# The beginning of a one-core transformer layer: who sums the tokens' squares, who copies the spread rows, and the order of the first loads

## The chip, the cores and the metric

The kernel runs on one core of one Trainium2 chip. The core has five engines, each with an instruction queue of its own that is worked off in order: TensorE (PE, matrix products; PEld are its weight loads), VectorE (DVE), ScalarE (ACT), GpSimd (POOL) and SyncE (SP), which here issues nearly all transfers from device memory. The metric is the device time of one execution in microseconds (us), the median of several runs. A profile shows one execution.

## The reference, cut to what matters

One layer with two token mixers and a gated MLP, on 512 latent tokens (`x`) and 256 context tokens (`ctx`), width 2048, everything in float32. What matters for this change is the modulated RMS norm ahead of the input projection:

```python
sc_ = jax.nn.silu(c)
scc = jax.nn.silu(c_ctx)
mod_x = (sc_ @ w_ada[l] + b_ada[l])[:, None, :]
mod_c = (scc @ w_ada[l] + b_ada[l])[None, None, :]
sh1, s1, g1, sh2, s2, g2 = jnp.split(mod_x, N_MOD, axis=-1)
sh1c, s1c, g1c, sh2c, s2c, g2c = jnp.split(mod_c, N_MOD, axis=-1)
...
h = _modulate(_rmsnorm(x, norm1_w[l]), sh1, s1)      # xn * (1 + s1) + sh1
hc = _modulate(_rmsnorm(xc, norm1_w[l]), sh1c, s1c)
q_da, k_da, v_da, q_mla, k_mla, v_mla = _mixer_inputs(h, tabs, *proj)
...
def _rmsnorm(x, w):
    xf = x.astype(jnp.float32)
    y = xf * lax.rsqrt(jnp.mean(xf * xf, axis=-1, keepdims=True) + EPS)
    return y.astype(x.dtype) * w
```

So each token needs the sum of its 2048 squares, and each of the 2048 features needs a shift and a scale for each of the two conditions `c` and `c_ctx`: products of `w_ada` with the two vectors.

## The kernel before, in words

Features lie on the 128 partitions, tokens along the free axis: `x_t[kt]` is feature tile kt (0 to 15) of the 512 latent tokens, `ctx_t` holds two tiles of the 256 context tokens in each block. A float32 product is made from three products of a high part (`wh`, `hh`) and a low part (`wl`, `hl`): `mm3`, lines 104 to 106.

The beginning, up to the first projection products, goes like this:

- Rows (lines 192 to 201). The two conditions are loaded as one row each, ACT takes their SiLU, PE multiplies a column of ones with the row (L199, four pieces of 512 for each condition), which spreads it over all partitions, and DVE copies the result from PSUM into `cb` and `ccb` (L200). Then ACT loads the function table that holds logarithm and exponential (`exp_ln_tables`, shown as L155).
- Squares (L266 to L284). For each feature tile, ACT squares the 512 latent columns (L276) and the 256 context columns (L277) into a tile `sq` of 768 columns. Even tiles are added to `sqs` by DVE (L279); odd tiles are summed over the partitions by PE with a matrix of ones into the PSUM tile `ssq` (L282, each set being products over 512 and 256 columns); at the end PE sums `sqs` as well (L284). The tag `h` has three buffers: `sqs` keeps one, so two turn.
- Root (`rstd`, L159 to L164). ACT takes logarithm and exponential, DVE corrects the result by one Newton step: `rinv`, one number for each token.
- Modulation, in rounds u of two feature tiles. `scales(u)` loads four blocks `adak` (0.5 MB each, four buffers) and multiplies them on PE with the conditions (`products`, L219), with a copy on ACT (L221), two small products (L223) and the result in `a1` (L235). `shifts(kt)` loads `ada[kt]` in two halves (0.5 MB each, five buffers). For even kt, DVE multiplies and sums each half with `cb` and `ccb`: four instructions (L251; the trace shows CUSTOM_DVE_ANT_0), the first half's and then the second half's, into one column of `modx` and `modc`. For odd kt, PE transposes the block (L258), ACT copies it (L259), and `products` does the rest (L262). `acc` is one PSUM bank that scales and odd shifts share.
- Projection. `w_g0[kt]` is loaded and split by ACT (L80) and DVE (L81). For each kt, DVE makes `h` from x, `a1` and `rinv` (L330), ACT adds the shift and keeps the high part (L332), DVE makes the low part (L333), and PE multiplies (L104 to L106). Round u + 1 of the modulation runs beside the products of round u.

After that stage (until about 183 us) come the other features, attention, the output projection and the MLP, which the change doesn't touch.

The order of the instructions on each engine is not that of the source. A planner fixes it before the run: it steps through a model of the engines and lets each one take, of the instructions that it holds ready, the one of the highest priority, which is that of the earliest line unless a block is marked `tc.high_priority()`. `tc.keep_in_program_order(i)` pins one instruction behind the instruction that was written last before it for the same engine; it isn't held back otherwise. On the chip each queue is then in order: an instruction that waits holds up all that stand behind it.

Of the kernel before, what the change touches and what calls it, by code (L numbers as in the profile page):

```python
# [9 lines left out]
F32 = mybir.dt.float32  # L10
# [3 lines left out]
ALU = mybir.AluOpType  # L14
# [3 lines left out]
P = 128  # L18
D = 2048
KT = D // P  # L20
T = 512
C = 256
TT = T + C
# [29 lines left out]
def layer_kernel(ctx: ExitStack, tc: tile.TileContext, small, rope, c_row, cc_row, x_t, ctx_t, ada, ada_k,  # L53
                 w_g0, w_f, w_v, w_uqn, w_uqr, w_ukv, w_o, w_up0, w_up, w_dn, out_t):
    nc = tc.nc
    pe, ve, sc, gp = nc.tensor, nc.vector, nc.scalar, nc.gpsimd
# [8 lines left out]
    def nm(s):  # L65
        n[0] += 1
        return f"{s}{n[0]}"

    def s_tile():
        return ps_s.tile([P, 1024], F32, tag="s", name=nm("s"))  # L70
# [3 lines left out]
    def b_tile(tag="b", bufs=None):  # L74
        return ps_b.tile([P, 512], F32, tag=tag, name=nm(tag), bufs=bufs or nb[0])

    def split(dst_h, dst_l, src, scale=None):

        if scale is None:
            sc.copy(dst_h, src)  # L80
            ve.tensor_tensor(dst_l, src, dst_h.bitcast(F32), op=ALU.subtract)  # L81
        else:
            sc.mul(dst_h, src, scale)
            ve.scalar_tensor_tensor(out=dst_l, in0=src, scalar=scale, in1=dst_h.bitcast(F32),
                                    op0=ALU.mult, op1=ALU.subtract)

    def wblock(src, cols=1024, pool=None):
        pool, full = (pool, cols) if pool else (wp, 1024)
        raw = pool.tile([P, full], F32, tag="wr", name=nm("wr"), bufs=3 if full == 1024 else 2)
        nc.sync.dma_start(raw[:, :cols], src)  # L90
        hi = pool.tile([P, full], F32R, tag="wh", name=nm("wh"), bufs=3)
        lo = pool.tile([P, full], F32R, tag="wl", name=nm("wl"), bufs=3)
        split(hi[:, :cols], lo[:, :cols], raw[:, :cols])
        return hi, lo
# [25 lines left out]
    def col(name, j=0):  # L120
        o = OFF[name] + j
        return smt[:, o:o + 1]
# [3 lines left out]
    ones32 = cst.tile([P, P], F32, name="ones32")  # L126
# [27 lines left out]
    def exp_ln_tables():  # L154
        tc.keep_in_program_order(sc.preload_act_table_set("natural_log_exp_and_others"))  # L155

    def rstd(out, ssq, dim, t1, t2):

        sc.activation(out, ssq, AF.Ln, bias=epst, scale=1.0 / dim)  # L159
        sc.activation(out, out, AF.Exp, scale=-0.5)  # L160
        ve.tensor_scalar(out=t1, in0=ssq, scalar1=1.0 / dim, scalar2=EPS, op0=ALU.mult, op1=ALU.add)
        ve.scalar_tensor_tensor(out=t2, in0=out, scalar=-0.5, in1=out, op0=ALU.mult, op1=ALU.mult)
        ve.tensor_tensor(t2, t2, t1, op=ALU.mult)
        ve.scalar_tensor_tensor(out=out, in0=t2, scalar=1.5, in1=out, op0=ALU.add, op1=ALU.mult)  # L164
# [12 lines left out]
    def a2k(dt=F32):  # L177
        return ap_.tile([P, 512], dt, tag="a2k", name=nm("a2k"))
# [3 lines left out]
    def c2k(dt=F32):  # L182
        return hcp.tile([P, 512], dt, tag="c2k", name=nm("c2k"))

    st = tc.alloc_tile_pool(name="st", bufs=1, reuse_waits="tile")
# [8 lines left out]
    for row, wide in ((c_row, cb), (cc_row, ccb)):  # L194
        nc.sync.dma_start(wide[0:1], row)
        sc.activation(wide[0:1], wide[0:1], AF.Silu)
        for j in range(0, D, 512):
            t = b_tile()
            pe.matmul(t, ones32[0:1], wide[0:1, j:j + 512], start=True, stop=True)  # L199
            ve.tensor_copy(wide[:, j:j + 512], t)  # L200
    exp_ln_tables()

    sel = sm.tile([P, 2], F32, name="sel")
# [9 lines left out]
    def products(src, n):  # L213
# [8 lines left out]
        for i in range(n // P):  # L222
            pe.matmul(acc[:, 2 * i:2 * i + 2], row[:, i * P:(i + 1) * P], sel, start=True, stop=True)  # L223

    def scales(u):

        ws = []
        for j in range(4):
            wk = st.tile([P, 4, 2 * P], F32, tag="adak", name=nm("adak"), bufs=4)
            nc.sync.dma_start(wk, ada_k[u, j // 2][:, (j % 2) * 4:(j % 2) * 4 + 4])  # L230
            ws.append(wk)
        products(lambda kt: ws[kt // 4][:, kt % 4], 2 * P)
        for i in range(2):
            kt = 2 * u + i
            ve.tensor_scalar(out=a1[:, 2 * kt:2 * kt + 2], in0=acc[:, 2 * i:2 * i + 2], scalar1=b1[:, kt:kt + 1],  # L235
                             scalar2=col("n1", kt), op0=ALU.add, op1=ALU.mult)

    def shifts(kt):


        ws = []
        for hf in range(2):
            w = st.tile([P, D // 2], F32, tag="ada", name=nm("ada"), bufs=5)
            nc.sync.dma_start(w, ada[kt][:, hf * D // 2:(hf + 1) * D // 2])
            ws.append(w)
        dst = [m[:, kt:kt + 1] for m in (modx, modc)]
        if kt % 2 == 0:
            for hf, w in enumerate(ws):
                for i, (vec, d) in enumerate(zip((cb, ccb), dst)):
                    t = w if i else st.tile([P, D // 2], BF16, tag="junk", name=nm("junk"), bufs=1)  # L250
                    ve.tensor_tensor_reduce(out=t, in0=w, in1=vec[:, hf * D // 2:(hf + 1) * D // 2], op0=ALU.mult,  # L251
                                            op1=ALU.add, scale=1.0, scalar=d if hf else col("b_ada", kt), accum_out=d)
            return
        wt = st.tile([P, KT, P], F32, tag="wt", name=nm("wt"), bufs=1)
        for q in range(4):
            for i in range(4):
                k = (q % 2) * 4 + i
                pe.transpose(acc[:, i * P:(i + 1) * P], ws[q // 2][:, k * P:(k + 1) * P], ident)  # L258
            sc.copy(wt[:, 4 * q:4 * q + 4].rearrange("p k f -> p (k f)"), acc)  # L259
        products(lambda kt: wt[:, kt], P)  # L260
        for i, d in enumerate(dst):
            ve.tensor_scalar(out=d, in0=acc[:, i:i + 1], scalar1=col("b_ada", kt), scalar2=None, op0=ALU.add)  # L262

    ssq = s_tile()
    sqs = st.tile([P, TT], F32, tag="h", name="sqs", bufs=3)
    xs, cs = [], []  # L266
    for kt in range(KT):
        xt = a2k()
        nc.sync.dma_start(xt, x_t[kt])
        xs.append(xt)  # L270
        if kt % 2 == 0:
            ct = c2k()
            nc.sync.dma_start(ct, ctx_t[kt // 2])
            cs.append(ct)
        sq = sqs if kt == 0 else st.tile([P, TT], F32, tag="h", name=nm("sq"), bufs=3)
        sc.square(sq[:, :T], xt)  # L276
        sc.square(sq[:, T:], cs[-1][:, (kt % 2) * C:(kt % 2 + 1) * C])  # L277
        if kt % 2 == 0 and kt:
            ve.tensor_tensor(sqs, sqs, sq, op=ALU.add)  # L279
        elif kt:  # L280
            for c0, c1 in ((0, T), (T, TT)):
                pe.matmul(ssq[:, c0:c1], ones32, sq[:, c0:c1], start=kt == 1, stop=False)  # L282
    for c0, c1 in ((0, T), (T, TT)):
        pe.matmul(ssq[:, c0:c1], ones32, sqs[:, c0:c1], start=False, stop=True)  # L284
    rinv = st.tile([P, TT], F32, name="rinv")
    nt2 = st.tile([P, TT], F32, tag="h", name="nt2", bufs=3)
    rstd(rinv, ssq[:, :TT], D, sqs, nt2)
    g0w = []

    def modulation(u):  # L290
        scales(u)
        for kt in (2 * u, 2 * u + 1):
            shifts(kt)
            g0w.append(wblock(w_g0[kt], 640, st))

    modulation(0)
    nc.sync.dma_start(silu_c, cb[0:1])
    nc.sync.dma_start(ropet, rope)
# [4 lines left out]
    for i in range(2):  # L303
        o = OFF["lam"] + 128 * i
        ve.tensor_tensor_reduce(out=lt, in0=smt[:, o:o + 64], in1=smt[:, o + 64:o + 128], op0=ALU.mult,
                                op1=ALU.add, scale=1.0, scalar=0.0, accum_out=ls[:, i:i + 1])
# [9 lines left out]
    for kt in range(KT):  # L316
        if kt % 2 == 0 and kt < KT - 2:
            modulation(kt // 2 + 1)
        ct = cs[kt // 2][:, (kt % 2) * C:(kt % 2 + 1) * C]
# [5 lines left out]
        with tc.high_priority():  # L325
            h = st.tile([P, TT], F32, tag="h", name=nm("h"), bufs=3)
            for i, (x, c, m, (hh, hl)) in enumerate(((xs[kt], slice(0, T), modx, hx[kt]),
                                                     (ct, slice(T, TT), modc, hc[kt]))):
                b, t, r = m[:, kt:kt + 1], h[:, c], rinv[:, c]
                ve.scalar_tensor_tensor(out=t, in0=x, scalar=a1[:, 2 * kt + i:2 * kt + i + 1], in1=r,  # L330
                                        op0=ALU.mult, op1=ALU.mult)
# [3 lines left out]
        for f in range(5):  # L335
            w = (wh[:, f * P:(f + 1) * P], wl[:, f * P:(f + 1) * P])
# [81 lines left out]
    for i in range(2):  # L418
        t = kv.tile([P, TT], F32, tag="lt", name=nm("ckv"), bufs=3)
# [27 lines left out]
    for i in range(3):  # L447
        lat = b_tile()
        feature(lat, None)
        t = kv.tile([P, TT], F32, tag="lt", name=nm("cq"), bufs=3)[:, :T]  # L450
# [4 lines left out]
    for half in range(2):  # L455
        s0, s1, b0, b1_ = s_tile(), s_tile(), b_tile(), b_tile()
        vo = [s0[:, :512], s0[:, 512:], s1[:, :512], s1[:, 512:], b0, b1_]
        for kb in range(8):
            wh, wl = next_block()
            for j in range(2):  # L460
                kt = kb * 2 + j
                w = (wh[:, j * 512:(j + 1) * 512], wl[:, j * 512:(j + 1) * 512])
                for t in range(NKEY):
                    src, o = (hx[kt], t * P) if t < 4 else (hc[kt], (t - 4) * P)
# [164 lines left out]
    for h in range(NH):  # L629
        i = h % 2  # L630
# [3 lines left out]
        for qt in range(NQT):  # L634
            c = slice(qt * P, (qt + 1) * P)
# [44 lines left out]
    for dt in range(KT):  # L680
        ve.scalar_tensor_tensor(out=a2[:, dt:dt + 1], in0=modx[:, 64 + dt:65 + dt], scalar=1.0,
                                in1=col("n2", dt), op0=ALU.add, op1=ALU.mult)
# [24 lines left out]
    for g in range(3):  # L707
# [5 lines left out]
        for kb in range(8):  # L713
            if g:
                next_gemv(wo, 1)
            w = wblock(w_o[g, kb])
# [19 lines left out]
    for ft in range(3, NFT):  # L736
        for k in range(7):
            jobs.append(("p", ft, k))
            c, n_ = ft // FC, (ft % FC) * 7 + k
# [46 lines left out]
    hf, hx, t1, t2, t3, t4 = ([None] * KT for _ in range(6))  # L786
# [599 lines left out]
```

## Time and profile before

| | us |
|---|---|
| median of three runs | 2444.63 (2444.59 to 2448.08) |
| the profiled execution | 2446.12 |
| its span | 2444.3 |

| engine | busy, share of the span |
|---|---|
| PE | 97% |
| PEld | 81% |
| DVE | 71% |
| ACT | 46% |
| POOL | 9% |

How to read the views: a group or an instruction is given with its engine, the source line (L276 is line 276), the operation, what it writes and reads with their shapes, and its time; where an engine stood idle before it, the releaser of the wait follows an arrow. In the chain of waits, each row is a piece of the work that ended last, found by going back from the end. `issue` is time for which the profile shows no wait. Queues of transfers are shown as SPq where SP issues them. The beginning up to 60 us is 2.5% of the span.

### The profile page before, as it was taken

Reading aid. Unit: us, or ns where it says so; the run is one execution under the profiler, and the core shown is the slowest. Engines: PE = TensorE matmul, PEld = TensorE weight load, DVE = VectorE, ACT = ScalarE, POOL = GpSimd, SP = SyncE. Lnnn points to the kernel's source line nnn. Section 1 sums busy time; section 2 is a strip of 40 time slices with the busy share of each in tenths; the row PEclk is TensorE's granted clock in tenths of the full one; section 3 lists DMA queues with packets and bytes.
Section 4 is the critical chain, followed back from the end, with each engine's and each line's share of the span. In section 5 each row is a group of like instructions: output and inputs, shape, how many; then the busy total and the mean of one; then the engine's idle time right before and its main releaser. Section 6 shows DMA issues by size and latency. Waiting matters only on the chain.

```text
span 2444.3 us, 32956 instructions
## 1 busy us (share of the span) xinstructions
PE 2374.6 (97%) x12790; PEld 1987.4 (81%) x12790; DVE 1730.4 (71%) x2304; ACT 1116.3 (46%) x1700; POOL 221.0 (9%) x244
## 2 busy tenths in 40 slices
PE   7999999999999999999999999999999999999998
PEld 3778887877777778889888888888888888888887
DVE  4668786388868877369766666666666666666667
ACT  4342121155545542245545454545454545454545
POOL 0000000121100002100111111111111111111110
PEclk9999999999999999999999999999999999999999
DMA  7867899555411139523555555565556555555573
GB/s 276 275 238 293 308 339 325 178 179 138 140 59 44 44 147 332 176 87 113 137 140 135 141 135 142 134 143 133 143 132 143 133 141 134 140 135 141 133 191 106
DMA packets 130708, 403.33 MB, mean 165 GB/s; under 512 B 14323, under 2 KB 25075, under 8 KB 122099
## 3 DMA queue, kind: packets, MB, share of 16 engines
q1 hardware_dynamic: 104118, 350.87, 43.8%
q0 software_dynamic: 25280, 49.30, 11.6%
q8 instruction: 100, 1.64, 0.3%
q10 hardware_dynamic: 1152, 1.05, 0.1%
q14 instruction: 58, 0.48, 0.1%
HBM read 331.68 MB, written 69.48 MB: 164 GB/s over the span
## 4 chain that ended last, share of the span: by engine, by line
PE 83%; DVE 8%; ACT 3%; DMA 3%; issue 2%; POOL 1%; SPq 0%; DVEq 0%; ACTq 0%; POOLq 0%
PE y L1105 12%; PE b L104 10%; PE b L105 10%; PE b L106 10%; PE z L1105 6%; PE y L1107 6%; PE z L1107 3%; PE s L104 3%; PE s L105 3%; PE s L106 3%; PE s L482 3%; PE x L1105 2%; DMA ada<-in_ada 1%; PE x L1107 1%; PE f L104 1%
## 5 line engine op out<-in xcount | busy, mean ns | idle before, releaser
L961 DVE TENSOR_TENSOR wl<-wr,wh 128x1024 fp32r<-128x1024 f32 x144 | 176.4, 1225 | 157.1 <-ACT wh L953 156.5
L953 ACT CAST wh<-wr 128x1024 fp32r<-128x1024 f32 x144 | 151.0, 1049 | 233.3 <-PE b L105 119.5
L104 PE MATMUL b<-ah,wh 128*128 128x512 f32 (+1 forms) x664 | 256.8, 387 | 0.0
L105 PE MATMUL b<-al,wh 128*128 128x512 f32 (+1 forms) x664 | 256.7, 387 | 0.0
L106 PE MATMUL b<-ah,wl 128*128 128x512 f32 (+1 forms) x664 | 255.8, 385 | 0.0
L1126 POOL DMA_DIRECT2D x_d<-xs x160 | 139.7, 1003 | 1161.1 <-ACT xs L1125 1158.7
L961 DVE TENSOR_TENSOR wl<-rb,wh 128x1024 fp32r<-128x1024 f32 x123 | 150.1, 1220 | 126.8 <-ACT wh L953 126.8
L953 ACT CAST wh<-rb 128x1024 fp32r<-128x1024 f32 x123 | 129.3, 1051 | 188.3 <-PE b L105 116.1
L961 DVE TENSOR_TENSOR wl<-ws,wh 128x1024 fp32r<-128x1024 f32 x123 | 150.2, 1221 | 89.7 <-ACT wh L953 89.7
L80 ACT CAST wh<-wr 128x1024 fp32r<-128x1024 f32 (+3 forms) x102 | 99.1, 972 | 219.1 <-PE b L106 61.7
L171 DVE CUSTOM_DVE_ANT_0 ada<-ada,cb,smt 128x2048 f32<-128x2048 f32 x64 | 153.4, 2397 | 59.3 <-DMA ada<-in_ada 59.0
L953 ACT CAST wh<-ws 128x1024 fp32r<-128x1024 f32 x123 | 128.2, 1042 | 129.7 <-DVE ws L915 48.6
L1105 PE MATMUL y<-a2k,wh 128*128 128x512 f32 x656 | 164.0, 392 | 0.0
L81 DVE TENSOR_TENSOR wl<-wr,wh 128x1024 fp32r<-128x1024 f32 (+3 forms) x102 | 118.0, 1157 | 53.4 <-ACT wh L80 53.1
L104 PE MATMUL b<-a2k,wh 128*128 128x512 f32 (+1 forms) x376 | 141.7, 377 | 5.9 <-ACT a2k L810 4.3
L106 PEld LDWEIGHTS b<-ah,wl 128*128 128x128 f32 x664 | 124.8, 188 | 25.7
L104 PEld LDWEIGHTS b<-ah,wh 128*128 128x128 f32 x664 | 125.1, 188 | 22.9
L105 PEld LDWEIGHTS b<-al,wh 128*128 128x128 f32 x664 | 125.1, 188 | 22.0
L105 PE MATMUL b<-a2k,wh 128*128 128x512 f32 (+1 forms) x376 | 140.5, 374 | 0.0
L106 PE MATMUL b<-a2k,wl 128*128 128x512 f32 (+1 forms) x376 | 139.3, 371 | 0.0
L1105 PEld LDWEIGHTS y<-a2k,wh 128*128 128x128 f32 x656 | 118.6, 189 | 21.6
L1105 PE MATMUL y<-b2k,wh 128*128 128x512 f32 x410 | 107.8, 393 | 0.0
(449 smaller groups left out, 5770.7 us busy)
## 6 DMA issues: line engine op xcount, KB each, us to landing
ada<-in_ada SPq DMA_DIRECT2D x64, 1024.0 KB, 6.7
rb<-in_w_up SPq DMA_DIRECT2D x123, 512.0 KB, 4.5
wr<-in_w_dn SPq DMA_DIRECT2D x88, 512.0 KB, 4.2
x_d<-xs POOLq DMA_DIRECT2D x160, 256.0 KB, 5.9
wr<-in_w_up SPq DMA_DIRECT2D x53, 512.0 KB, 4.2
wr<-in_w_f SPq DMA_DIRECT2D x34, 512.0 KB, 6.4
adak<-in_ada_k SPq DMA_DIRECT2D x32, 512.0 KB, 6.0
ada<-in_ada SPq DMA_DIRECT2D x32, 512.0 KB, 6.4
```

Of the source, the lines that this page charges most:

```text
L80: sc.copy(dst_h, src)
L81: ve.tensor_tensor(dst_l, src, dst_h.bitcast(F32), op=ALU.subtract)
L104: pe.matmul(out, st[0], mv[0], start=start, stop=False, **kw)
L105: pe.matmul(out, st[0], mv[1], start=False, stop=False, **kw)
L106: pe.matmul(out, st[1], mv[0], start=False, stop=stop, **kw)
L171: ve.tensor_tensor_reduce(out=junk, in0=w, in1=vec, op0=ALU.mult, op1=ALU.add, scale=1.0, scalar=col("b_ada", j), accum_out=dst[:, j:j + 1])
L482: pe.matmul(s[:, c0:c1], a, b[:, c0:c1], start=i == 0, stop=i == len(mms) - 1)
L953: sc.copy(t, raw[:, k * n_:k * n_ + n_])
L961: ve.tensor_tensor(t, raw[:, k * n_:k * n_ + n_], hi[k].bitcast(F32), op=ALU.subtract)
L1105: pe.matmul(o, w[j][0], hs[j], start=start and j == 0, stop=False, skip_group_check=True)
L1107: pe.matmul(o[:, h0], w[j][1], hs[j][:, h0], start=False, stop=j == 7, skip_group_check=True)
L1126: gp.dma_start(x1_d[dt], x, accum_op=ALU.add)
```

## The change

- The eight copies of the spread rows (`cb`, `ccb`) go from DVE to ACT; the table load, pinned behind what was written before it on ACT, now comes behind the last of them.
- The square of the context columns goes from ACT to DVE. DVE adds tiles 1 to 13 to `sqs` (before: the even tiles 2 to 14); PE sums only `sqs` and the tiles 14 and 15. The loop and its loads are marked as of high priority, and the loads are pinned in written order.
- The first shift (`shifts(0)`) is written ahead of the root and ahead of `scales(0)`; its loads come before those of `scales(0)`, and its first instruction on DVE is pinned behind the last square. The root is marked as of high priority and gets two scratch tiles of its own.
- In the later rounds the even shift is written ahead of the scales; before, the scales came first.

```diff
         for j in range(0, D, 512):
             t = b_tile()
             pe.matmul(t, ones32[0:1], wide[0:1, j:j + 512], start=True, stop=True)
-            ve.tensor_copy(wide[:, j:j + 512], t)
+            sc.copy(wide[:, j:j + 512], t)
     exp_ln_tables()
...
+    def load(i, dst, src):
+        t = nc.sync.dma_start(dst, src)
+        if i == 0:
+            tc.keep_in_program_order(t)
+
     def scales(u):
...
-            nc.sync.dma_start(wk, ada_k[u, j // 2][:, (j % 2) * 4:(j % 2) * 4 + 4])
+            load(u, wk, ada_k[u, j // 2][:, (j % 2) * 4:(j % 2) * 4 + 4])
...
-            nc.sync.dma_start(w, ada[kt][:, hf * D // 2:(hf + 1) * D // 2])
+            load(kt, w, ada[kt][:, hf * D // 2:(hf + 1) * D // 2])
...
-                    ve.tensor_tensor_reduce(out=t, in0=w, in1=vec[:, hf * D // 2:(hf + 1) * D // 2], op0=ALU.mult,
-                                            op1=ALU.add, scale=1.0, scalar=d if hf else col("b_ada", kt), accum_out=d)
+                    r = ve.tensor_tensor_reduce(out=t, in0=w, in1=vec[:, hf * D // 2:(hf + 1) * D // 2], op0=ALU.mult,
+                                                op1=ALU.add, scale=1.0, scalar=d if hf else col("b_ada", kt),
+                                                accum_out=d)
+                    if kt == hf == i == 0:
+                        tc.keep_in_program_order(r)
...
-    for kt in range(KT):
-        xt = a2k()
-        nc.sync.dma_start(xt, x_t[kt])
-        xs.append(xt)
-        if kt % 2 == 0:
-            ct = c2k()
-            nc.sync.dma_start(ct, ctx_t[kt // 2])
-            cs.append(ct)
-        sq = sqs if kt == 0 else st.tile([P, TT], F32, tag="h", name=nm("sq"), bufs=3)
-        sc.square(sq[:, :T], xt)
-        sc.square(sq[:, T:], cs[-1][:, (kt % 2) * C:(kt % 2 + 1) * C])
-        if kt % 2 == 0 and kt:
-            ve.tensor_tensor(sqs, sqs, sq, op=ALU.add)
-        elif kt:
-            for c0, c1 in ((0, T), (T, TT)):
-                pe.matmul(ssq[:, c0:c1], ones32, sq[:, c0:c1], start=kt == 1, stop=False)
-    for c0, c1 in ((0, T), (T, TT)):
-        pe.matmul(ssq[:, c0:c1], ones32, sqs[:, c0:c1], start=False, stop=True)
-    rinv = st.tile([P, TT], F32, name="rinv")
-    nt2 = st.tile([P, TT], F32, tag="h", name="nt2", bufs=3)
-    rstd(rinv, ssq[:, :TT], D, sqs, nt2)
+    with tc.high_priority():
+        for kt in range(KT):
+            xt = a2k()
+            tc.keep_in_program_order(nc.sync.dma_start(xt, x_t[kt]))
+            xs.append(xt)
+            if kt % 2 == 0:
+                ct = c2k()
+                tc.keep_in_program_order(nc.sync.dma_start(ct, ctx_t[kt // 2]))
+                cs.append(ct)
+            sq = st.tile([P, TT], F32, tag="h", name=nm("sq"), bufs=3) if kt else sqs
+            c = cs[-1][:, (kt % 2) * C:(kt % 2 + 1) * C]
+            sc.square(sq[:, :T], xt)
+            ve.tensor_tensor(sq[:, T:], c, c, op=ALU.mult)
+            if kt and kt < KT - 2:
+                ve.tensor_tensor(sqs, sqs, sq, op=ALU.add)
+            if kt == KT - 3:
+                for c0, c1 in ((0, T), (T, TT)):
+                    pe.matmul(ssq[:, c0:c1], ones32, sqs[:, c0:c1], start=True, stop=False)
+            elif kt >= KT - 2:
+                for c0, c1 in ((0, T), (T, TT)):
+                    pe.matmul(ssq[:, c0:c1], ones32, sq[:, c0:c1], start=False, stop=kt == KT - 1)
     g0w = []
 
     def modulation(u):
+        if u:
+            shifts(2 * u)
         scales(u)
-        for kt in (2 * u, 2 * u + 1):
-            shifts(kt)
-            g0w.append(wblock(w_g0[kt], 640, st))
-
+        g0w.append(wblock(w_g0[2 * u], 640, st))
+        shifts(2 * u + 1)
+        g0w.append(wblock(w_g0[2 * u + 1], 640, st))
+
+    shifts(0)
+    with tc.high_priority():
+        rinv = st.tile([P, TT], F32, name="rinv")
+        nt1, nt2 = (st.tile([P, TT], F32, tag="h", name=nm("nt"), bufs=3) for _ in range(2))
+        rstd(rinv, ssq[:, :TT], D, nt1, nt2)
     modulation(0)
```

## The prediction

> **What bounds the kernel now.** First the page: its span and its busy times.
>
> ```profile
> span 2444.3 us, 32956 instructions
> PE 2374.6 (97%) x12790; PEld 1987.4 (81%) x12790; DVE 1730.4 (71%) x2304; ACT 1116.3 (46%) x1700; POOL 221.0 (9%) x244
> ```
>
> TensorE sets the time nearly everywhere, so an edit of the beginning is worth what it takes from the idle or half-speed time of PE there. Second, the busy time by stretches, of which one stands for those behind it (stretch and its length in us; busy us of PE, PEld, DVE, ACT, POOL; granted clock, DMA share, GB/s).
>
> ```profile
> 80.00:100.00 20.00, 20.00 (x186) 14.88 (x185) 13.10 (x26) 8.37 (x16) 0.00 (x0) 1.00 0.82 282
> ```
>
> From 80 us on PE has no idle time and the transfers have room (DMA share 0.82). So what happens before 80 us moves all that follows by the same amount, and nothing behind it gives more or takes it back. Third, the chain of work that ended last, in order of time (start, length, what).
>
> ```profile
> 7.08 14.01 PE b L199 x16
> 21.09 5.43 PE s L282 x8
> 26.55 0.64 ACT sq L276
> 27.23 1.57 PE s L282 x4
> 28.82 0.64 ACT sq L276
> ...
> 40.17 1.30 PE s L284 x4
> ...
> 46.51 1.20 DVE junk L251
> ...
> 52.28 0.73 ACT a2k L332
> 53.05 1.22 PE s L104 x2
> ```
>
> Four stretches precede the first projection product (L104, 53.05). Rows: PE spreads the two conditions' rows, 7.08 to 21.09. Squares: there are two turning buffers, so PE frees one, ACT squares into it, PE sums it; that costs 27.23 to 28.82 and so on, 2.28 us for each pair of feature tiles, up to S = 41.47. Root: S to 46.51. Shift: the three products of L251 that the shift's column needs, then ACT's first h at 52.28.
>
> The transfers are not the limit there (same columns as above):
>
> ```profile
> 30.00:32.00 2.00, 1.28 (x5) 0.60 (x4) 0.96 (x1) 1.49 (x5) 0.00 (x0) 1.00 1.01 412
> ...
> 34.00:36.00 2.00, 1.56 (x4) 0.68 (x4) 0.83 (x1) 1.49 (x5) 0.00 (x0) 1.00 0.01 2
> ```
>
> At 34 us everything asked for has landed and the DMA engines stand still.
>
> **The change part by part.** The rows needed (first six groups of the view by form: busy us, mean ns of one; then the timeline: start, length, engine, line).
>
> ```profile
> L279 DVE TENSOR_TENSOR sqs<-sqs,sq 128x768 f32<-128x768 f32 x7 | 6.7, 957 | 10.8 <-ACT sq L277 10.8
> L259 ACT COPY wt<-b 128x512 f32<-128x512 f32 x4 | 2.3, 581 | 4.5 <-PE b L258 4.5
> L81 DVE TENSOR_TENSOR wl<-wr,wh 128x640 fp32r<-128x640 f32 x2 | 1.6, 824 | 0.0
> L330 DVE SCALAR_TENSOR_TENSOR h<-a2k,a,rinv 128x512 f32<-128x512 f32 x2 | 1.4, 750 | 0.0
> L251 DVE CUSTOM_DVE_ANT_0 ada<-ada,ccb,smt 128x1024 f32<-128x1024 f32 x1 | 1.3, 1284 | 0.0
> L330 DVE SCALAR_TENSOR_TENSOR h<-c2k,a,rinv 128x256 f32<-128x256 f32 x2 | 0.9, 484 | 0.0
> ```
>
> ```profile
> 8.84 1.28 ACT L155 ACT_TABLE_LOAD   x1
> 10.14 0.63 ACT L276 ACTIVATE sqs<-a2k 128x512 f32<-128x512 f32 x1
> ...
> 12.32 0.40 ACT L277 ACTIVATE sq<-c2k 128x256 f32<-128x256 f32 x1
> ...
> 16.01 0.69 DVE L200 COPY ccb<-b 128x512 f32<-128x512 f32 x1 [1.02 <-PE b L199]
> ...
> 16.62 0.95 DVE L279 TENSOR_TENSOR sqs<-sqs,sq 128x768 f32<-128x768 f32 x1
> ```
>
> 1. The sum moves from PE to DVE. Removed: five of the eight PE sets (one: four products over 768 columns), and ACT's ctx squares (0.40 each, the row of 12.32). Added on DVE: sixteen ctx squares (128x256) and six more 128x768 adds (13 against 7). The ctx square has no row. Bounds: a third of the 768 add, 0.32, and the two-input 128x256 row, 0.48; I take 0.42, from the line through the two TENSOR_TENSOR rows (640 elements 0.824, 768 elements 0.957: 1.04 ns each and 0.16). DVE then needs 0.42 + 0.96 = 1.38 us a feature tile where a pair took 2.28, and the loop through PE is gone.
>
> Earliest end: the squares of tiles 0 and 1 follow Silu at 8.84, where the table load stood, done at 10.1; 13 adds and 12 ctx squares, 13 x 0.957 + 12 x 0.42 = 17.5, give 27.6; three sets at 1.57 make S = 32.3.
>
> 2. The copies of the spread rows move to ACT, 0.58 each, and the table load is now pinned behind the last of them. PE's pace is unchanged, so the eighth copy ends at about 21.1 + 0.6 = 21.7, and the load at 23.0. Queued behind copies that wait for PE stand the squares. How many, no view shows; the order is fixed by a planner before the run. The old order on DVE gives a hint: tile 2's add (16.62) was put behind the fifth copy (16.01), though its square was done at 12.7, when PE, at 14.01 / 8 = 1.75 a copy, had fed three. The planner therefore takes the rows for faster than they are, and in the new order some six to eight of the sixteen squares should stand ahead of the eighth copy, the rest behind. With tiles 0 to 7 ahead: square 8 ends at 23.0 + 0.63 = 23.6; adds 8 to 13 and five ctx squares are 6 x 0.957 + 5 x 0.42 = 7.8, to 31.5. PE has stood still since 21.1, so I take two sets at the pace of the first eight products (5.43 / 2 = 2.72) and one at 1.57: 7.0. S = 38.5, 3.0 earlier. This is nearest to the rows, so I take it; 32.3 stays as the other end.
>
> The load took 1.28 and the next ACT instruction began 0.02 behind it. [...]
>
> PE's row products ran 14 us without a break and the sets behind them still took 2.72 each, those from 27.23 on 1.57. [...]
>
> 3. Root, S to rinv: 5.0 as before (41.47 to 46.51); its two scratch tiles are new, but the third buffer is free by then.
>
> 4. First shift's products. They took three times 1.28 between rinv and the first h, with the multiplications for h among them: rinv to L104 was 6.5. Now the weights land ahead of the scales' blocks and the four products are pinned behind the last ctx square, at about 32. By the chip's time all four (5.1) fit before S = 38.5, when the root can begin. But the root has high priority, so the planner may put the others behind it. Bounds: none behind the root, 1.5 (0.75 for h's multiplication, 0.73 for ACT's h); three behind, 1.5 + 3.9 = 5.4. I take two behind, the middle: 4.0, a gain of 2.5. First product: 38.5 + 5.0 + 4.0 = 47.5 against 53.05: 5.5.
>
> 5. Loads. The ada_k blocks wait for 1 MB of ada more, 2.5 us at the 412 GB/s above; but all of the first round is in by 34 in any order, 4 us before the scales' products can follow S. In later rounds ada comes ahead of ada_k in SP's queue:
>
> ```profile
> 38.52 4.85 SPq L230 DMA_DIRECT2D adak<-in_ada_k  x4
> 43.42 7.97 SPq L244 DMA_DIRECT2D ada<-in_ada  x2
> ```
>
> PE's rows for this step and the next:
>
> ```profile
> 48.81 1.12 PE L258 MATMUL b<-ident,ada 128*128 128x128 f32 x4 [0.68 <-ACT wt L259]
> ...
> 59.65 0.64 PE L219 MATMUL b<-adak,cpad 128*32 128x256 f32 x8
> ...
> 73.41 0.66 PE L258 MATMUL b<-ident,ada 128*128 128x128 f32 x4 [0.68 <-ACT wt L259]
> 74.86 1.22 PE L104 MATMUL s<-a2k,wh 128*128 128x512 f32 x2 [0.80 <-ACT a2k L332]
> ```
>
> ada's second half of tile 2 waited until 51.4 for a buffer that the first shift's products free. In the new order the four ada_k stand behind that wait, until the second product is done, about 45 to 48; 2 MB then take 5 us, in by 53. Their use at 59.65 is 6.6 behind L104, so 54.1 in the new time: hidden by a us. If that cover goes, it costs what it lacks, 2 us at most.
>
> 6. From the first product to 80 us. Three of tile 1's four groups of transposes, the last of them at 48.81, lay in the wait before 53.05. With that wait shorter, and ada of tile 1 later in the queue, they may fall behind L104: a loss of 0 to 2.0 (three groups at the 0.66 of the later row). Against it, PE waited 0.68 + 0.80 = 1.5 around tile 2's first product, where the shift again came last; shifts now go ahead of scales, a gain of 0 to 1.5. I set the two against each other: 0, bounds 2 either way.
>
> Sum: 3.0 + 2.5 + 0 = 5.5. The profiled execution took 2446.12 (span 2444.3 and 1.8 around it), so 2440.6; the median of three is 1.5 below it, 2444.63, which gives 2439.1, say 2439.
>
> **The rivals.**
>
> All of it comes (B). ACT's queue doesn't hold the squares and the four products fit: S about 34 (27.6 and two cold sets and one warm, 34.6), root 5.0, h 1.5: L104 at 41. That is 12 earlier, less some 1 to 2 at tile 1: 10.5, 2434. For it: data lands in time, and DVE is free 10.8 us waiting for squares today. Against: the five copies ahead of tile 2's add.
>
> The change doesn't do what it says (C). Six squares ahead of the copies (S = 39.9) and three shift products behind the root (5.4): L104 at 50.3, 2.8 earlier, and tile 1's transposes take 2 back: about 1, 2443.5. For it: high priority for the root, and ACT's order; against: at tile 2 the shift no longer comes last.
>
> Slower (D), ACT's queue: the planner puts all eight copies ahead of the squares. Each feature tile that falls behind the eighth copy costs 1.38. With only tile 0 squared before it, 13 adds remain: 23.6 + 13 x 0.957 + 12 x 0.42 + 7.0 = 48.1, root 5.0, shift 5.4: L104 at 58.5, 5.5 later, 2450. It decides from about tile 4: with tiles 0 to 4 ahead, nine adds remain, S = 42.6, and L104 falls at 53.0, as now. Against: squares have high priority, and at 10.14 the first of them waited for nothing but its turn on ACT.
>
> **How the numbers follow.** This kernel's measurement tells 0.2% (4.9 us) from no change. Forecast A, 5.5 less, with its own bounds 2 to 9: 0.45, of which I put 0.27 beyond 4.9 and 0.18 within. B 0.25, all faster. C 0.19, within, with a little slack. D 0.11, slower. Faster 0.52, same 0.37, slower 0.11. Range: from B's upper half, 2431, to between C and D, 2447; left out are the best of B and D.
>
> **What would show it.** Step 1: no ACT wait on PE for square buffers, three sets of L282's kind only, DVE adds 1.4 us apart. Step 2: the count of squares ahead of the eighth copy on ACT; the table load among the squares; S at 38.5. Step 4: how many L251 lie between the root's last step and the first L330. Step 5: SP's ada_k of round 1 issued at 45 to 48 and landed before their products. Step 6: L104 at 47.5, and PE without idle time from 80 us less that gain. I am wrong if S comes later than 41.5, if L104 moves and the end doesn't, or if a stage past 180 us changes its length.

## The result, and the profile after

The changed kernel took 2446.9 us in the median of 14 runs (2443.51 to 2448.85), the kernel before 2444.06 in 14 runs beside it (2440.51 to 2448.08). The ratio is 1.001 with a 95% interval of 1.0002 to 1.0018: some 0.1% slower, where 0.2% faster was forecast. The profiled execution took 2446.22 us.

Page of the changed kernel, span and busy times; little of either has moved:

```profile
span 2444.5 us, 32907 instructions
PE 2368.8 (97%) x12766; PEld 1979.5 (81%) x12766; DVE 1732.5 (71%) x2318; ACT 1117.3 (46%) x1692; POOL 220.5 (9%) x244
```

Three places of the trace tell the story: S, which is the end of the squares' sum on PE; the first projection product (L104); and a marker at the end of this stage, the second of the sets of column sums that follow the projection (L407 before, L423 after). Here is the chain of waits of the changed kernel, from the last add to the first product and then at the marker (start, length, what):

```profile
32.01 0.96 DVE sqs L290
...
33.02 2.93 PE s L293 x4
35.94 1.71 PE s L296 x2
37.65 1.01 PE b L219 x8
38.66 1.69 PE s L296 x4
40.35 0.57 PE b L219 x8
40.92 0.64 PE s L296 x2
...
41.59 0.91 ACT rinv L159
...
190.07 1.52 PE s L423 x4
```

And the marker in the chain of waits of the kernel before:

```profile
188.79 1.52 PE s L407 x4
```

PE's timeline of the changed kernel has the first product here:

```profile
50.13 1.20 PE L104 MATMUL s<-a2k,wh 128*128 128x512 f32 x2
```

The sum on VectorE ended at 32.97, but S still stands at 41.55 (41.47 before): the three sets took 8.5 us, and two groups of eight scale products (L219) ran between them. L104 starts at 50.13 against 53.05, 2.9 earlier. The marker is 1.3 *later* (190.03 against 188.76 on PE's timeline). So the stretch from the first product to the marker grew by 4.2 us, and that is where the gain went.

On ScalarE (timeline: start, length, engine, line, operation, tiles; in brackets the idle time ahead and what ended it):

```profile
18.18 0.63 ACT L287 ACTIVATE sq<-a2k 128x512 f32<-128x512 f32 x1
...
21.11 0.58 ACT L200 COPY ccb<-b 128x512 f32<-128x512 f32 x1 [1.12 <-PE b L199]
21.60 0.63 ACT L287 ACTIVATE sq<-a2k 128x512 f32<-128x512 f32 x1
22.25 1.28 ACT L155 ACT_TABLE_LOAD   x1
...
48.72 0.58 ACT L267 COPY wt<-b 128x512 f32<-128x512 f32 x1 [1.21 <-PE b L266]
49.20 0.72 ACT L348 ACTIVATE a2k<-h,modx 128x512 fp32r<-128x512 f32 x1
```

The square at 18.18 is that of tile 5, the sixth; the seventh stands behind the eighth copy, at 21.60. The last two rows show what stood ahead of the first h (a2k, 49.20): the copy of a transpose of tile 1, which waited for PE. On VectorE the shift's four products were all done before the root, the first of them here, and a weight's low part (wl) slipped in behind rinv:

```profile
33.34 1.28 DVE L256 CUSTOM_DVE_ANT_0 junk<-ada,cb,smt 128x1024 bf16<-128x1024 f32 x1
...
37.19 1.28 DVE L256 CUSTOM_DVE_ANT_0 ada<-ada,ccb,modc 128x1024 f32<-128x1024 f32 x1
...
45.65 0.95 DVE L164 SCALAR_TENSOR_TENSOR rinv<-nt,rinv 128x768 f32<-128x768 f32 x1
46.51 0.82 DVE L81 TENSOR_TENSOR wl<-wr,wh 128x640 fp32r<-128x640 f32 x1
```

What follows the first product? The stretch that answers to the one shown of before (windows: stretch and length; busy us of PE, PEld, DVE, ACT, POOL with instruction groups; granted clock, DMA share, GB/s):

```profile
80.00:100.00 20.00, 20.00 (x167) 13.75 (x167) 12.28 (x24) 6.38 (x12) 0.00 (x0) 1.00 0.81 290
```

PE is busy for 20.00 of 20 us at a granted clock of 1.00, as before. Yet the weight loads fill 13.75 us where they filled 14.88 (71.78 against 77.53 us from 80 to 180 us): less work was done in the same full busy time. The rows that close a round of scales (four products of sel) measure how much. Before, PE's timeline, rounds 2 and 7:

```profile
83.81 0.54 PE L223 MATMUL b<-sel,row 128*128 128x2 f32 x4
...
162.79 0.54 PE L223 MATMUL b<-sel,row 128*128 128x2 f32 x4
```

After, the same two:

```profile
85.16 0.50 PE L223 MATMUL b<-sel,row 128*128 128x2 f32 x4
...
169.05 0.53 PE L223 MATMUL b<-sel,row 128*128 128x2 f32 x4
```

Five rounds (3 to 7) take 78.98 us before and 83.89 after: 15.80 and 16.78 each, 4.9 us lost in five rounds, all at "100% busy". PE's timeline shows what differs within a round. A round has 32 scale products (sixteen calls, two instructions each in the trace). Before, they all stand together from round 3 on (in four groups in round 1, in two in round 2):

```profile
96.66 0.28 PE L104 MATMUL b<-c2k,wh 128*128 128x256 f32 x1
96.78 0.28 PE L105 MATMUL b<-c2k,wh 128*128 128x256 f32 x1
96.99 1.93 PE L219 MATMUL b<-adak,cpad 128*32 128x256 f32 x32
98.85 0.39 PE L106 MATMUL b<-c2k,wl 128*128 128x256 f32 x1
99.08 0.40 PE L105 MATMUL s<-a2k,wh 128*128 128x512 f32 x1
```

After, they stand in four groups of eight between the projection's products in all of the rounds 1 to 7. One of the groups:

```profile
133.79 0.39 PE L106 MATMUL s<-a2k,wl 128*128 128x512 f32 x1
134.02 0.28 PE L104 MATMUL b<-c2k,wh 128*128 128x256 f32 x1
134.22 0.64 PE L219 MATMUL b<-adak,cpad 128*32 128x256 f32 x8
134.79 0.39 PE L105 MATMUL b<-c2k,wh 128*128 128x256 f32 x1
135.01 0.28 PE L106 MATMUL b<-c2k,wl 128*128 128x256 f32 x1
135.13 0.40 PE L105 MATMUL s<-a2k,wh 128*128 128x512 f32 x1
```

Such rows are read from start to start, since the modelled ends overlap. A 256-column product takes 0.12 among its like (96.66 to 96.78), but 0.21 ahead of a group (96.78 to 96.99), 0.20 in the second fence, and 0.23 or 0.22 behind one. So each group costs its neighbours about 0.2. And eight products take 0.57 (134.22 to 134.79), four groups 2.28, where 32 together take 1.86. Three groups more at 0.19 and 0.42 for the products themselves are 1.0 us a round: the 0.98 measured. This was a reading of two traces; the experiments test it.

### The profile page after: what moved, and what is told of

The parts are those of the page before. It is cut to its first block, busy times and chain, and to the rows that moved or that the text cites. A ratio compares the mean times of both kernels' runs of the same rounds, so it can differ in the third digit from the quotient of the medians.

```text
span 2444.5 us, 32907 instructions
## 1 busy us (share of the span) xinstructions
PE 2368.8 (97%) x12766; PEld 1979.5 (81%) x12766; DVE 1732.5 (71%) x2318; ACT 1117.3 (46%) x1692; POOL 220.5 (9%) x244
## 4 chain that ended last, share of the span: by engine, by line
issue 50%; PE 32%; POOL 7%; DVE 6%; DMA 3%; ACT 2%; SPq 0%; POOLq 0%; DVEq 0%; ACTq 0%
POOL x_d L1142 6%; PE b L105 3%; PE b L106 3%; PE b L104 3%; PE s L104 3%; PE s L105 3%; PE s L106 3%; PE s L498 3%; DMA ada<-in_ada 1%; PE f L104 1%; PE pt L510 1%; DVE m L500 1%; PE b L219 1%; PE f L105 1%; PE f L106 1%
## 5 line engine op out<-in xcount | busy, mean ns | idle before, releaser
L104 PE MATMUL b<-ah,wh 128*128 128x512 f32 (+1 forms) x664 | 256.8, 387 | 0.0
L171 DVE CUSTOM_DVE_ANT_0 ada<-ada,cb,smt 128x2048 f32<-128x2048 f32 x64 | 151.4, 2365 | 51.7 <-DMA ada<-in_ada 51.3
L104 PE MATMUL b<-a2k,wh 128*128 128x512 f32 (+1 forms) x376 | 141.6, 377 | 5.9 <-ACT a2k L826 4.3
L104 PEld LDWEIGHTS b<-ah,wh 128*128 128x128 f32 x664 | 125.1, 188 | 22.9
```

The lines of the kernel that those rows point to most:

```text
L104: pe.matmul(out, st[0], mv[0], start=start, stop=False, **kw)
L171: ve.tensor_tensor_reduce(out=junk, in0=w, in1=vec, op0=ALU.mult, op1=ALU.add, scale=1.0, scalar=col("b_ada", j), accum_out=dst[:, j:j + 1])
```

## The experiments

All ten kernels, with before and after. "Stretch" runs from the first L104 to the marker. It is split with windows of 1 us: lost clock is the sum of (1 - granted clock) x length, idle is length less PE's busy time, and the rest is what is left, PE's work at full clock. (Idle time at a lowered clock counts in both, so the rest is up to a us too low.)

| kernel | first L104 | marker | stretch | lost clock | idle | rest | median us, ratio to before (95%) |
|---|---|---|---|---|---|---|---|
| before | 53.05 | 188.76 | 135.7 | 3.9 | 5.0 | 126.8 | 2444.06 |
| after | 50.13 | 190.03 | 139.9 | 3.0 | 4.3 | 132.6 | 2446.9, 1.001 (1.0002 to 1.0018) |
| e1_scales_first | 49.28 | 187.73 | 138.5 | 5.8 | 6.3 | 126.3 | 2442.02, 0.9993 (0.9984 to 1.0002) |
| e2_last_piece_first | 49.41 | 182.48 | 133.1 | 4.1 | 4.0 | 125.0 | 2438.49, 0.9978 (0.9969 to 0.9987) |
| e2b_last_piece_first_all | 48.64 | 180.79 | 132.2 | 2.0 | 4.0 | 126.2 | 2434.82, 0.9968 (0.9957 to 0.9979) |
| e3_before_shift_first | 53.14 | 191.82 | 138.7 | 2.3 | 3.6 | 132.8 | 2445.13, 1.001 (1.0002 to 1.0019) |
| e7_two_groups | 49.94 | 184.02 | 134.1 | 2.7 | 3.9 | 127.4 | 2439.89, 0.9991 (0.9982 to 0.9999) |
| e5_copies_on_dve | 50.93 | 186.31 | 135.4 | 2.3 | 2.1 | 131.0 | 2441.31, 0.9991 (0.9982 to 1.0) |
| e6_one_group_one_set | 48.10 | 180.23 | 132.1 | 1.9 | 4.0 | 126.2 | 2436.33, 0.9972 (0.9961 to 0.9983) |
| e8_one_group_one_set_dve_copies | 47.49 | 177.98 | 130.5 | 1.1 | 3.5 | 125.9 | 2433.18, 0.9959 (0.9947 to 0.9971) |
| e10_before_one_group | 53.98 | 187.82 | 133.8 | 3.7 | 4.9 | 125.3 | 2441.96, 0.9992 (0.9982 to 1.0001) |
| e12_scales_first_one_group | 48.62 | 185.71 | 137.1 | 3.7 | 6.3 | 127.0 | 2442.95, 0.9991 (0.9982 to 1.0001) |

The kernel before had medians of 2442.97, 2442.9 and 2442.96 in the three sets of runs that these were compared in (e1 to e3; e5 to e8; e10 and e12). Behind the marker the profiled executions take 2250 to 2258 us in an order that follows no edit, so a place is read from a profile, and a gain of a us or two only from the medians. The first L104 has a spread of its own: e1, e2 and e7 leave round 0 as the change has it, and it lies at 49.28, 49.41 and 49.94 there against 50.13. In e2, for one, the eight scale products behind the second set's first half take 0.57 (37.49 to 38.06) where the change's take 1.01. A difference of under a us in that column is not put down to an edit here.

**Which part of the change splits the scale products?** The scales first again, as before, with all else of the change kept:

```
     def modulation(u):
-        if u:
-            shifts(2 * u)
         scales(u)
+        if u:
+            shifts(2 * u)
```

> The changed kernel, with one thing put back: in rounds 1 to 7 scales(u) is written ahead of shifts(2u), as before the change. Theory 1 (splitting): in the changed kernel the 32 products of a round's scales (L219) stand on PE in four groups of 8 between projection products, where before they stood in one group of 32; by the PE rows a group of 32 takes 1.86 us, four of 8 take 2.17, and each change from one to the other costs the product ahead and the product behind some 0.08 and 0.10 more, 0.84 us a round, 5.9 over seven rounds. Here the planner puts them in one group from round 3 on (2 and 1 groups in rounds 2 and 3), so a round takes about 16 us again instead of 16.9, the products behind the stage (L423, at 190.1 in the changed kernel) start at about 184 to 186, and the time is 2441 to 2443, some 4 to 5 us below the changed kernel and 1 to 3 below the kernel before. Theory 2 (the order of loads and DVE's earlier products stretch the round, however the products are grouped): the same gain here. Theory 3 (the round is as long as before and the lead of the first product is given back behind the stage): no change, 2447.

The round came back (15.84 us) and the rest of the stretch fell from 132.6 to 126.3, so the order of the two calls makes the groups. But the marker is only 2.3 earlier than the change's. What was saved went into a wait: tile 2's shift comes last again (PE's timeline of this kernel),

```profile
73.02 1.22 PE L104 MATMUL s<-a2k,wh 128*128 128x512 f32 x2 [2.66 <-ACT a2k L348]
```

and the windows behind it show PE at a granted clock of 0.50:

```profile
72.00:74.00 2.00, 0.98 (x2) 0.83 (x3) 1.96 (x5) 1.75 (x4) 0.00 (x0) 0.50 0.89 296
74.00:76.00 2.00, 2.00 (x8) 1.65 (x7) 1.34 (x3) 0.91 (x3) 0.00 (x0) 0.50 0.79 227
76.00:78.00 2.00, 2.00 (x23) 1.40 (x26) 0.00 (x0) 0.15 (x1) 0.00 (x0) 0.51 0.98 373
```

**The groups joined without touching the order of the calls.** The sum over 16 row tiles is taken with the last piece of the weights first, so that the planner has no scale product ready before that piece is due. In e2 for rounds 1 to 7, in e2b for all:

```
-                kt = 4 * j + c
+                kt = 4 * (3 - j if back else j) + c
...
-        products(lambda kt: ws[kt // 4][:, kt % 4], 2 * P)
+        products(lambda kt: ws[kt // 4][:, kt % 4], 2 * P, u > 0)
```

> The changed kernel, with the 32 products of each later round's scales taken from the last-loaded block to the first, so that the first of them waits for the whole load and all 32 stand together on PE; loads, their order and all other work as in the changed kernel. Theory 1 (splitting): the round falls from 16.9 to about 16 us, the products behind the stage start at about 184 instead of 190.1, and the time is about 2441, 5 to 6 below the changed kernel, 3 below the kernel before. Theory 2 (order of loads and of DVE's products): nothing changes, 2447. Theory 3: nothing changes.

> As e2_last_piece_first, in round 0 as well. In the changed kernel two groups of eight of round 0's scales stand between the three sets of the squares' sum (1.01 and 0.57 us), so the sum ends at 41.55. Theory 1 for the start: with the 32 behind the sets the sum ends 1.6 earlier, at about 40, and the first projection product comes at about 48.5 to 50 instead of 50.1; time about 2440 (0 to 1.5 below e2_last_piece_first). If the first product waits for something else (the transposes' copies ahead of it on ACT, 48.7), the time is that of e2_last_piece_first.

Rounds took 15.71 and 15.72 us, and both kernels beat before: 0.9978 (0.9969 to 0.9987) and 0.9968 (0.9957 to 0.9979). The amount of arithmetic is the same as in the changed kernel, and SyncE issues the loads in the same order, so a round stretched by the new order of loads is ruled out. What the edit changes is the place of the 32 products in PE's queue, and by the ratios it is worth 0.32% (8 us) against the change in e2 and 0.42% (10 us) in e2b. In e2b the groups between the three sets are gone too (PE's timeline):

```profile
33.08 2.93 PE L293 MATMUL s<-sqs,ones 128*128 128x512 f32 x4 [11.94 <-DVE sqs L290]
35.80 4.31 PE L296 MATMUL s<-sq,ones 128*128 128x512 f32 x8
40.04 1.93 PE L219 MATMUL b<-adak,cpad 128*32 128x256 f32 x32
```

The sets now take 7.0 us, and S comes at 40.11 in place of 41.55. e2 and e2b have the same three waits at tile 2 (0.55, 0.63 and 0.68 us), but not the same clock behind them. e2:

```profile
68.00:70.00 2.00, 1.47 (x6) 1.38 (x7) 2.00 (x5) 1.81 (x4) 0.00 (x0) 0.50 0.78 172
70.00:72.00 2.00, 2.00 (x11) 1.68 (x10) 1.39 (x3) 1.01 (x3) 0.00 (x0) 0.67 1.00 392
```

e2b:

```profile
68.00:70.00 2.00, 2.00 (x14) 1.66 (x14) 1.69 (x5) 1.93 (x4) 0.00 (x0) 1.00 0.85 225
70.00:72.00 2.00, 2.00 (x14) 1.60 (x12) 1.99 (x3) 1.09 (x2) 0.00 (x0) 1.00 1.01 404
```

**The same order of calls in the kernel before, alone:**

```
-        scales(u)
-        for kt in (2 * u, 2 * u + 1):
-            shifts(kt)
-            g0w.append(wblock(w_g0[kt], 640, st))
+        if u:
+            shifts(2 * u)
+        scales(u)
+        if not u:
+            shifts(2 * u)
+        g0w.append(wblock(w_g0[2 * u], 640, st))
+        shifts(2 * u + 1)
+        g0w.append(wblock(w_g0[2 * u + 1], 640, st))
```

> The kernel before, with one part of the change: in rounds 1 to 7 shifts(2u) is written ahead of scales(u). The planner then splits the 32 products in four groups in every later round. Theory 1 (splitting) and theory 2 (order of loads) both say a round of about 16.9 us instead of 16 and a time about 4 to 6 above the kernel before, 2448 to 2450 (the first product of tile 2 may come some us earlier, which takes part of it back); theory 3 says no change, 2444.

The round takes 16.78, as in the changed kernel, and the rest 132.8. With the beginning as it was (L104 at 53.14), the marker falls 3.1 later than before, and the ratio is 1.001 (1.0002 to 1.0019). So this part of the change costs by itself, in either beginning. The rest grows by 6.0 here and by 5.8 in the change; part of it is won back as shorter waits and less lost clock at tile 2, and the time stays below the 2448 to 2450 that was expected.

**Two groups of sixteen**, by another order of the four pieces in rounds 1 to 7:

```
+    def products(src, n, order=(0, 1, 2, 3)):
...
+                kt = 4 * order[j] + c
...
+        products(lambda kt: ws[kt // 4][:, kt % 4], 2 * P, (1, 0, 3, 2) if u else (0, 1, 2, 3))
```

> The changed kernel, with the four loaded blocks of each later round's scales taken in the order 2nd, 1st, 4th, 3rd, so that the 32 products stand on PE in two groups of 16 (four of 8 in the changed kernel, one of 32 in e2_last_piece_first). Theory 1 (each change from one kind of product to the other costs PE time): with four groups a round takes 16.78 us (85.16 to 169.05 over five rounds), with one 15.71 (82.93 to 161.48), 0.36 for each further group, so here 16.07 us a round and a time 2.5 above e2_last_piece_first, about 2441. Rival (waiting for the last block, or the order in which the sums are taken, is what helps, not the number of changes): 15.7 as in e2 or 16.8 as in the changed kernel.

One group gives 15.7 us a round, two 15.97, four 16.78; the rest is 125.0 in e2, 127.4, and 132.6. It rises with the number of groups, though by more from two to four (0.81) than from one to two (0.26). The time of 2439.89 lies between e2's and the change's, as the cause asks.

**Why S came late: the queue of ScalarE?** The copies of the spread rows back on VectorE:

```
-            sc.copy(wide[:, j:j + 512], t)
+            ve.tensor_copy(wide[:, j:j + 512], t)
```

> The changed kernel with the eight copies of the spread rows back on DVE; ACT's squares then stand behind no copy. Theory Q (ACT's queue holds the squares behind the copies): the last add into the running sum ends at about 30 instead of 32.96 (six adds and six context squares stand behind the eighth copy, now on DVE itself, from 21.9 on), the squares' sum ends at about 38.5 to 39 instead of 41.55, and the time is 2 to 3 below the changed kernel, 2444 to 2445. Rival (PE's half pace and the scales' products between its sets set that end): the last add comes earlier, but the sum's end stays at 41 to 41.5 and the time at 2447. The round stays at 16.8 us in both.

The squares were then free of the copies, but the last add ended only 0.8 earlier (32.15), since the copies now stood in the adds' own queue; S came 1.3 later (42.86) and L104 0.8 later, which neither expectation had. This run does not test ScalarE's queue alone: PE's order moved too, and 20 scale products came to stand inside the first set.

```profile
32.20 2.07 PE L293 MATMUL s<-sqs,ones 128*128 128x512 f32 x2 [11.14 <-DVE sqs L290]
34.20 2.78 PE L219 MATMUL b<-adak,cpad 128*32 128x256 f32 x20
```

What the copies' place is worth to S is read from e6 and e8 below, where all scale products stand behind the sum: 0.7 us. Still the kernel is faster than the change, by the two ratios (0.9991 against 1.001) and by 3.7 us at the marker. PE's timeline gives a reading of why, which was not tested further:

```profile
46.99 0.66 PE L266 MATMUL b<-ident,ada 128*128 128x128 f32 x4 [0.68 <-ACT wt L267]
48.32 1.62 PE L219 MATMUL b<-wt,cpad 128*32 128x128 f32 x32 [0.67 <-ACT wt L267]
50.31 0.59 PE L223 MATMUL b<-sel,row 128*128 128x2 f32 x2 [0.36 <-ACT row L221]
50.93 1.22 PE L104 MATMUL s<-a2k,wh 128*128 128x512 f32 x2
```

All of tile 1's transposes and their products stand ahead of the first L104, in PE's idle time; in the change they stand partly behind it. Idle time in the stretch is 2.1 where the change has 4.3.

**Fewer sets on PE.** On e2b, tiles 14 and 15 are also added on VectorE, and one set remains; e8 has the copies on VectorE besides:

```
-            if kt and kt < KT - 2:
+            if kt:
                 ve.tensor_tensor(sqs, sqs, sq, op=ALU.add)
-            if kt == KT - 3:
+            if kt == KT - 1:
                 for c0, c1 in ((0, T), (T, TT)):
-                    pe.matmul(ssq[:, c0:c1], ones32, sqs[:, c0:c1], start=True, stop=False)
...
+                    pe.matmul(ssq[:, c0:c1], ones32, sqs[:, c0:c1], start=True, stop=True)
```

> e2b_last_piece_first_all, and tiles 14 and 15 added on DVE as well, so that PE sums over the partitions with one set instead of three. The two more adds with their context squares cost 2 x 1.38 on DVE, two sets at half pace 5.4 to 5.6 on PE are gone. Theory (the end of the sum is the last add plus the sets at half pace): the sum ends at 33.0 + 2.8 + 2.9 = 38.7 instead of 40.13, the first projection product comes 1.4 earlier, time about 2433.5. Rival (the first product waits for round 0's scales or the transposes' copies on ACT): 2435 as e2b.

> e6_one_group_one_set with the copies back on DVE, so that no square waits behind a copy on ACT. Theory Q: the last add ends at about 33 instead of 35.8 and the sum at 36 instead of 38.7, time about 2431. Rival (something else gates the first projection product): 2433 to 2435, as e6.

e6 has S at 38.55, 1.6 earlier than e2b, yet its first L104 comes only 0.5 earlier (48.10), so S alone no longer sets it. Its time is not below e2b's (2436.33 and 2434.82, with intervals that overlap). e8 has S at 37.87 and L104 at 47.49, and the lowest median of the study: 2433.18, 0.9959 (0.9947 to 0.9971), with an interval that overlaps those of e6 and e2b.

**What the rest of the change is worth once the groups are joined.** The last piece first, put into the kernel before (e10), and into e1, where the scales come ahead of the shift (e12):

```
-        products(lambda kt: ws[kt // 4][:, kt % 4], 2 * P)
+        products(lambda kt: ws[kt // 4][:, kt % 4], 2 * P, True)
```

> The kernel before, with only the blocks of each round's scales taken from the last to the first, so that every round's 32 products stand in one group (before: two groups in round 0, four in round 1, two in round 2, one from round 3 on). Theory 1: five changes fewer at 0.3 to 0.36 us, 1.5 to 1.8, of which round 0's may be hidden: 2441 to 2442, and what e2b_last_piece_first_all has beyond that (about 6.5 us) is worth of the change's other parts. Rival (the grouping alone gives what e2b_last_piece_first_all gives, and the change's other parts are worth nothing): 2435.

> e1_scales_first with the blocks taken from the last to the first in every round: all rounds in one group, the start as in e2b_last_piece_first_all, only the scales ahead of the even shifts in the later rounds. In e1 PE waited 2.66 us for tile 2's shift (73.02) and ran at half pace about there (granted clock 0.66 between 70 and 80 us). Theory W (shifts ahead of scales are worth that wait and the half pace): the wait stays here and the time is about 2440, 5 above e2b_last_piece_first_all. Rival (the order of shifts and scales matters only through the grouping): 2435.

e10 gains next to nothing (0.9992, 0.9982 to 1.0001), since before had its 32 products in one group from round 3 on already. So most of e2b's 8 us against before is the change's own. And e12 has the early beginning (L104 at 48.62, as e2b) and single groups, but at 0.9991 (0.9982 to 1.0001) keeps almost nothing of it (2442.95, above both expectations). Against e2b its stretch is 4.9 longer: 2.4 of idle time, 1.7 of lost clock, 0.8 of the rest. PE waits 1.96 us there for tile 2's first h (L104 at 71.66), a wait that the shift-first order takes away. That its median lies no lower than e10's, though its marker is 2.1 earlier, is not explained.

## Why the prediction was wrong

**The step that failed** is the opening claim that "nothing behind it gives more or takes it back", and with it the 0 of step 6. Steps 5 and 6 weighed the new order of shifts and scales by its transfers, tile 1's transposes and tile 2's wait alone. The order also moved the scale products on PE, from one group to four, and that took back 1.0 us in each of the rounds 3 to 7 (4.9 together), where before had one group; round 2 had two and round 1 four already. Step 6 was set at 0 with bounds of 2; measured from the first product to the marker it is a loss of 4.2: 5.8 more work time, less 0.7 of idle time and 0.9 of lost clock. The busy share could not have warned: it is 100% with either grouping. What could were the rows of before: 0.21 us for a product next to a group where its like takes 0.12, and the group of only eight at 59.65, quoted in step 5, in a round that was split before the change too. The reordered calls went through a planner that orders every engine's queue, and PE's queue had not been considered. Two of the prediction's own signs of being wrong came: S later than 41.5 (41.55), and a first product that moved while the end did not.

**Step 1 held.** No square waits for a buffer that PE frees, and adds come in pairs every 2.6 us, 1.3 a tile (forecast 1.4). One set of L293 and two of L296 remain.

**Step 2 was mis-sized.** It expected six to eight squares ahead of the eighth copy and took eight; there were six. The last add ended at 32.97 in place of 31.5. The sets took 8.5 in place of 7.0, because two groups of the scales' products (1.01 and 0.57) went between them; where they are gone (e2b) the sets take 7.0, as estimated. So S came at 41.55 and not 38.5, and this gain of 3.0 was nothing. In the change, the first eight scale products between the sets took 1.01 (from 37.65) and the next eight 0.57 (from 40.35), at a granted clock of 1.00 from 33 to 42 us; what set that pace no run shows. The square behind the table load began 0.01 after the load's end (at 23.54).

**Step 3 held:** root 5.0 (41.55 to 46.6).

**Step 4 had nearly the right size for another reason.** It put two shift products behind the root, 4.0 us from rinv to L104. All four were done before the root, as rival B had it, but the path was still 3.5: the weight's low part on VectorE (0.82) and a transpose's copy on ScalarE stood ahead of h. In sum L104 came 2.9 earlier, where 5.5 was forecast and rival C had 2.8.

**Step 5 had the result right and the wait wrong.** The loads were hidden: round 1's products never waited for one. But the later loads of ada_k did not stand behind ada's second half until 45 to 48, since the shift's products came ahead of the root; they were issued from 38.72 on, once the first eight scale products had run (SyncE's timeline of the changed kernel).

```profile
38.72 4.27 SPq L226 DMA_DIRECT2D adak<-in_ada_k  x4
```

**The rivals.** B's bare 1.5 behind the root and D's queue of copies did not come; the cold and warm sets that B counts are sets of 2.72 and 1.57, the rows of before, and three took 8.5 in the change and 7.0 in e2b. C came nearest, with the first product where it put it (50.3, measured 50.13), but by luck. Its S of 39.9 does not follow from step 2: six squares ahead, at 1.38 for each of the two tiles less, make 41.3, and with its own root and shift L104 at 51.7; with six squares ahead the change measured 41.55. And C took 2 us from tile 1's transposes, where the rounds 3 to 7 alone lost 4.9. The result lies just inside the top of the range (2447); that is luck as well, since the range ended there on account of D's queue of copies.

With the groups joined the change gives about what was forecast, and more (8 us in e2b; about 7 of it, 8.2 less e10's 1.0, by the change's own parts). That is not the forecast's mechanism come true: S is 1.4 earlier there, not 3.0, and part of the gain comes from the wait and the lost clock at tile 2.

## What to carry to other kernels

When an edit changes the order in which work is handed to a planner, compare PE's order of products round by round, and count how often products of another kind break into a run: here a busy share of 100% hid that cost, and the time from one round's closing row to the next showed it. If a sum can be taken in any order, asking first for the piece that comes last keeps its products together. And a gain at the beginning counts only at the end of its stage: read a marker there, not only the first product.

## What the runs showed of the hardware

Breaking a run of projection products for a group of scale products cost PE about 0.2 us a time at a granted clock of 1.00 (and the 32 products themselves took 2.28 in four groups, 1.86 in one), and PE showed no idle time for it (busy 100.00 us from 80 to 180 us in the change, 99.88 before); PEld's busy time is what fell (71.78 against 77.53 us in the same stretch). The two kinds differ in the columns of the weights held (32 and 128) and in type (f32 and fp32r); which of the two it is was not tried.

The clock lost between 62 and 84 us had three values: 0 in e2b, e3, e5, e6 and e8; 1.7 us in before, after, e2, e7, e10 and e12; 3.42 in e1. In windows of 1 us the granted clock there was 0.50 (in e2 from 68 to 71 us, in e1 from 72 to 77). With the same three waits at tile 2 (0.55, 0.63 and 0.68 us) e2b lost nothing and e2 1.7 us. Why was not shown, and whether the loss changes from run to run of one kernel can't be told from one profile of each.
